# Feed-forward matmuls of a two-block transformer on one core: two matmuls of 256 columns, high weight part by high and by low activations, become one of 512

## The chip, the cores and the metric

The kernel runs on one core of a Trainium2 chip. The metric is the device time of one execution in microseconds (us); the median of several runs is given. TensorE does the matmuls (PE in the profile, its weight loads PEld), VectorE (DVE) and ScalarE (ACT) the elementwise work, GpSimd (POOL) a little of it, and the queue of SyncE (SP) starts nearly all DMA transfers.

## What is computed

Two transformer blocks follow each other, each of two layers, at model width 1024. All values are fp32. The second block works on the latents `x` (256 tokens) and on a context of 256 tokens, which its first layer carries along; its last layer updates the latents alone.

```
def first_block(x, ...):
    for l in range(2):
        h = rms_norm(x, norm_mix_pre[l])
        x = x + rms_norm(hybrid_mixer(h, ...), norm_mix_post[l])
        h = rms_norm(x, norm_ffn_pre[l])
        x = x + rms_norm(swiglu(h, w_ffn_in[l], w_ffn_out[l]), norm_ffn_post[l])
    return x

def swiglu(h, w_in, w_out):
    g, up = jnp.split(h @ w_in, 2, axis=-1)
    return (jax.nn.silu(g) * up) @ w_out

def conv_ffn(h, P):                      # feed-forward part of second_block
    gt = dwconv(h @ P["w_gate"], P["ffn_conv_w"], P["ffn_conv_b"])
    return (jax.nn.silu(gt) * (h @ P["w_val"])) @ P["w_down"]
```

The hidden width of each feed-forward part is 2816, or 22 groups of 128. The second block also needs `silu(c) @ w_mod`, six rows of 1024 for each layer, from 24 MB of weights a layer.

## The kernel before

**Products in parts.** An fp32 product is made of three matmuls in a narrower format. Every weight tile `raw` (128 x 1024, 512 KB) is split into a rounded high part `hi` and the remainder `lo`; so are the activations (`hThi`, `hTlo`). `mm3` issues high by high (L508), high by low (L509) and low by high (L510) into one PSUM accumulator. In the rows below the right-hand side of an arrow names the moving operand and the weights: `mm<-hTlo,hi` is L509.

**The weight stream.** `Stream` brings one 128 x 1024 tile for each projection, in the order of use. The load goes out on SP's queue (L262, six `raw` buffers), ACT makes `hi` (L275) and DVE makes `lo` (L278); there are four buffers each for `hi` and `lo`. The split is issued three tiles ahead, so that the `lo` of tile k + 3 stands on DVE's list near the work of projection k.

**The feed-forward input.** `ffn_in` goes over the 22 hidden groups. For each it makes two projections, `g` and `up`: 8 steps of 128 along the model width, three matmuls of 256 columns each step. Both 256-token results share one PSUM bank of 512 columns. `swiglu_unit` turns them into the hidden values: a tanh on ACT (L833), two operations on DVE (L834, L835, tile `tt`), and the split into `hh` (ACT, L840) and `hl` (DVE, L841). `convffn_unit`, in the second block, does the same with a convolution of three taps.

Three stages have this form with 256 tokens: the first block's layer 0 (406 to 546 us of the trace, called f1 below), its layer 1 (1035 to 1183 us, f2) and the second block's layer 1 (1963 to 2091 us, s1). Each has 44 projections, called P0 to P43. The second block's layer 0 works on 512 tokens and has 512-column matmuls already.

**What else runs in them.** In f1 and f2 the generator `mods` is woven in. It multiplies the `w_mod` tiles (`wm`, two buffers, loaded on SP's queue at L1142) by a column of the condition, and adds them up on DVE in two accumulators `macc` (L1169 for the first tile of a row, L1171 for the seven others; four instructions of 512 columns for each tile). When the eight tiles of a row are added, PE sums over the partitions (`am`, L1177), transposes (L1187), and DVE writes the result to `kept` (L1190); rows 2 and 5 then go to DRAM as `md`, in DMAs on POOL's queue (L1195). In f2 attention and a convolution of the second block's context run too (`cv`, `on`, `cn`, `yl`).

**What sets the order.** The program is written as above; a scheduler then puts the instructions of each engine in one fixed list, by readiness and priority. Every engine works through its list in that order and waits on semaphores, so an instruction that waits holds up all that stand behind it. PSUM's eight banks are handed out by the same scheduler.

Of the kernel before, what the change touches and what calls it, by code (L numbers as in the profile page):

```python
# [10 lines left out]
FR = mybir.dt.float32r  # L11
AF = mybir.ActivationFunctionType
# [121 lines left out]
class Pack:  # L134
    def __init__(self):
        self.at = {}
        self.n = 0
        self.items = []
# [160 lines left out]
class Kern:  # L299
# [30 lines left out]
    def __init__(self, nc, tc, ctx, dr, stop=None):  # L330
        self.nc, self.tc, self.dr = nc, tc, dr
        self.stop = stop
        e = ctx.enter_context
        self.cp = e(tc.tile_pool(name="const", bufs=1))
        self.wp = e(tc.tile_pool(name="wts", bufs=4))
        self.sp = e(tc.tile_pool(name="slots", bufs=self.NSLOT))
        self.tp = e(tc.tile_pool(name="tmp", bufs=3))
        self.mp = e(tc.tile_pool(name="psmm", bufs=4, space=PSUM))
        self.ap = e(tc.tile_pool(name="psax", bufs=4, space=PSUM))
        self.dp = e(tc.tile_pool(name="scratch", bufs=1, space=bass.MemoryType.DRAM))  # L340
        self.x = self.cp.tile([128, 2, D], F32, name="x")
        self.xc = self.cp.tile([128, 2, D], F32, name="xc")
        cpk = const_params()
        kept = self.cp.tile([128, cpk.n + KEEP], F32, name="kept")
        self.kept, self.kept_n = kept, 0
        self.ident, cst, self.tabs, self.ctp, self.ct, self.ones, self.nh, self.par_f = (
            self.keep(n) for n in (128, cpk.n, 512, 256, 16, 1, 1, 240))
        self.cst_all, self.cst = cst, {n: cpk.get(cst, n) for n in cpk.at}
        for t in range(2):
            for h in range(2):  # L350
                sl = slice(512 * h, 512 * h + 512)
                nc.sync.dma_start(self.x[:, t, sl], dr["x"][128 * t:128 * t + 128, sl])
        nc.sync.dma_start(self.ident, dr["ident"])
        nc.gpsimd.memset(self.ones, 1.0)
        nc.gpsimd.memset(self.nh, -0.5)
        self.par = {}
        self.uid = 0
        self.lanes = [[] for _ in range(7)]
        self.lo_pool = 0
        self.front = []  # L360
        self.P2, self.late, self.ctx_out, self.tails = None, [], {}, []
        self.filler, self.filled = None, 0
        layers = [(dr[f"w_f{l}"], first_units(l)) for l in range(2)] + [(dr[f"w_s{l}"], second_units(l)) for l in range(2)]
        self.st = Stream(self, layers)
# [70 lines left out]
    def norm_acts(self, ntok):  # L435
        per = 1024 // ntok
        out = []
        for _ in range(8 // per):
            hi, lo = self.slot("hThi", FR), self.slot("hTlo", FR)
            for k in range(per):  # L440
                o = slice(ntok * k, ntok * k + ntok)
                out.append((hi[:, o], lo[:, o]))
        return out
# [68 lines left out]
    def proj_T(self, key, ps, acts, nk=8, width=128, m=0, part=None):  # L512
        hi, lo = self.st.next(key) if part is None else part
        for k in range(nk):
            o = k * width + 128 * m
            self.mm3(ps, (hi[:, o:o + 128], lo[:, o:o + 128]), acts[k], k == 0, k == nk - 1)

    def proj_T_held(self, keys, pss, acts, order):
        parts = [self.st.next(key, hold=True) for key in keys]
# [282 lines left out]
    def ffn_in(self, hT, part, fn, side=1):  # L802
        ntok = hT[0][0].shape[-1]
        per = 1024 // ntok
        hid, hi, lo = [], None, None
        done = {}
        if ntok == 512 and part[0] == 0:
            done = {("g", 0): self.mm_ps(), ("up", 0): self.mm_ps(), ("g", 1): self.mm_ps()}
            self.proj_T_held(list(done), list(done.values()), hT, (1, 0))
        for i, m in enumerate(part):  # L810
            if i % per == 0:
                hi, lo = self.slot("hh", FR), self.slot("hl", FR)
            pg = done.get(("g", m)) or self.mm_ps()
            pu = done.get(("up", m)) or (pg[:, 256:] if ntok == 256 else self.mm_ps())
            pg = pg[:, :ntok]
            if ("g", m) not in done:
                self.proj_T(("g", m), pg, hT)
            if ("up", m) not in done:
                self.proj_T(("up", m), pu, hT)
            o = slice(ntok * (i % per), ntok * (i % per) + ntok)  # L820
            fn(m, pg, pu, hi[:, o], lo[:, o])
            hid.append((hi[:, o], lo[:, o]))
            self.run_side(side)
            if ntok == 512:
                self.fill(2 if self.filled < 64 else 3)
            elif i % 4 < 3 and self.filled < 48:
                self.fill(1)
        return hid
# [993 lines left out]
```

## Time and profile before

| | |
|---|---|
| median of 3 runs | 2151.7 us (2150.6 to 2153.8) |
| profiled execution | 2158.38 us, span 2156.2 us |
| mean granted TensorE clock | 0.983 of full speed |
| PE busy | 2071.8 us, 96% of the span |
| DVE busy | 1557.3 us, 72% |
| ACT busy | 1070.1 us, 50% |
| f1, f2, s1: first to last matmul | 406.05 to 546.24, 1034.98 to 1183.07, 1963.42 to 2091.38 us |

The span reaches from the first instruction to the last one; the profiled execution took 2.2 us more than that, and 6.7 us more than the median. The shares are means over stages that differ, so the rows of one stage say more than the table.

### The profile page before, as it was taken

Reading aid. Unit: us, or ns where it says so; the run is one execution under the profiler, and the core shown is the slowest. Engines: PE = TensorE matmul, PEld = TensorE weight load, DVE = VectorE, ACT = ScalarE, POOL = GpSimd, SP = SyncE. Lnnn points to the kernel's source line nnn. Section 1 sums busy time; section 2 is a strip of 40 time slices with the busy share of each in tenths; the row PEclk is TensorE's granted clock in tenths of the full one; section 3 lists DMA queues with packets and bytes.
Section 4 is the critical chain, followed back from the end, with each engine's and each line's share of the span. In section 5 each row is a group of like instructions: output and inputs, shape, how many; then the busy total and the mean of one; then the engine's idle time right before and its main releaser. Section 6 shows DMA issues by size and latency. Waiting matters only on the chain.

```text
span 2156.2 us, 34229 instructions
## 1 busy us (share of the span) xinstructions
PE 2071.8 (96%) x13088; PEld 1801.9 (84%) x13088; DVE 1557.3 (72%) x2823; ACT 1070.1 (50%) x1900; POOL 293.8 (14%) x271
## 2 busy tenths in 40 slices
PE   8999999999999999999799987999989999899999
PEld 6788899898887898998799876687868888678997
DVE  7756656897579466569997489789865546977774
ACT  5555644644455556457545474643313335455552
POOL 2101112100032011121300045100000002610000
PEclk9999999999999999999899999899999999999999
DMA  8545566687655454557566744256873233324553
GB/s 308 159 137 174 179 199 196 208 233 252 201 175 165 147 157 130 174 169 251 158 204 170 249 139 152 100 158 196 232 226 107 73 105 108 97 83 144 186 186 117
DMA packets 102356, 366.67 MB, mean 170 GB/s; under 512 B 12560, under 2 KB 12720, under 8 KB 102192
## 3 DMA queue, kind: packets, MB, share of 16 engines
q1 hardware_dynamic: 99920, 358.65, 52.8%
q0 software_dynamic: 2272, 5.83, 1.0%
q8 instruction: 103, 1.69, 0.3%
q14 instruction: 61, 0.50, 0.1%
HBM read 361.76 MB, written 2.68 MB: 169 GB/s over the span
## 4 chain that ended last, share of the span: by engine, by line
PE 84%; DVE 9%; DMA 3%; issue 2%; ACT 1%; POOL 0%; SPq 0%; POOLq 0%; DVEq 0%; ACTq 0%
PE mm L508 25%; PE mm L510 25%; PE mm L509 25%; DMA wm<-in_w_mod 2%; DVE cv L1504 2%; DVE lo L278 2%; DVE macc L1171 2%; PE ax L1312 1%; PE ax L937 1%; PE ax L1342 1%; ACT hi L275 1%; PE am L1158 1%; PE ay L461 1%; PE ay L590 1%; PE ax L892 1%
## 5 line engine op out<-in xcount | busy, mean ns | idle before, releaser
L275 ACT ACTIVATE hi<-raw 128x1024 fp32r<-128x1024 f32 (+1 forms) x564 | 592.9, 1054 | 765.8 <-PE mm L509 382.1
L278 DVE TENSOR_TENSOR lo<-raw,hi 128x1024 fp32r<-128x1024 f32 (+2 forms) x552 | 694.7, 1261 | 373.8 <-ACT hi L275 366.6
L508 PE MATMUL mm<-hThi,hi 128*128 128x256 f32 (+1 forms) x2408 | 723.1, 302 | 14.6 <-DVE gz L1291 12.1
L510 PE MATMUL mm<-hThi,lo 128*128 128x256 f32 (+1 forms) x2408 | 717.2, 299 | 4.6 <-DVE lo L278 4.5
L509 PE MATMUL mm<-hTlo,hi 128*128 128x256 f32 (+1 forms) x2408 | 719.6, 300 | 0.5 <-DVE hTlo L471 0.5
L508 PEld LDWEIGHTS mm<-hThi,hi 128*128 128x128 f32 x2408 | 460.2, 192 | 44.6 <-issue 13.6
L510 PEld LDWEIGHTS mm<-hThi,lo 128*128 128x128 f32 x2408 | 461.0, 192 | 24.2 <-DVE lo L278 5.0
L509 PEld LDWEIGHTS mm<-hTlo,hi 128*128 128x128 f32 x2408 | 462.5, 192 | 15.3 <-issue 1.7
L509 PE MATMUL mm<-lo,hThi 128*128 128x512 f32 (+2 forms) x480 | 182.4, 381 | 9.7 <-DVE lo L278 9.7
L508 PE MATMUL mm<-hi,hThi 128*128 128x512 f32 (+2 forms) x480 | 181.7, 386 | 5.2 <-DVE rb L579 3.1
L1171 DVE SCALAR_TENSOR_TENSOR macc<-wm,kept,macc 128x512 f32<-128x512 f32 x224 | 161.8, 763 | 31.5 <-DMA wm<-in_w_mod 31.3
L510 PE MATMUL mm<-hi,hTlo 128*128 128x512 f32 (+2 forms) x480 | 180.2, 378 | 0.0
L508 PE MATMUL mm<-hi,hh 128*128 128x512 f32 x440 | 173.1, 394 | 4.2 <-DVE xn L1564 4.2
L509 PE MATMUL mm<-lo,hh 128*128 128x512 f32 x440 | 173.2, 394 | 3.1 <-DVE lo L278 3.1
L510 PE MATMUL mm<-hi,hl 128*128 128x512 f32 x440 | 172.6, 393 | 0.0
L509 PEld LDWEIGHTS mm<-lo,hThi 128*128 128x128 f32 x480 | 90.9, 190 | 28.3 <-DVE lo L278 12.4
L508 PEld LDWEIGHTS mm<-hi,hThi 128*128 128x128 f32 x480 | 90.9, 190 | 26.4 <-issue 6.9
L510 PEld LDWEIGHTS mm<-hi,hTlo 128*128 128x128 f32 x480 | 90.5, 189 | 16.3 <-issue 0.3
L508 PEld LDWEIGHTS mm<-hi,hh 128*128 128x128 f32 x440 | 83.6, 190 | 22.4 <-issue 5.0
L509 PEld LDWEIGHTS mm<-lo,hh 128*128 128x128 f32 x440 | 83.7, 190 | 21.0 <-DVE lo L278 3.6
L510 PEld LDWEIGHTS mm<-hi,hl 128*128 128x128 f32 x440 | 83.7, 190 | 17.7
L1504 DVE SCALAR_TENSOR_TENSOR cv<-yp,kept,cv 128x256 f32<-128x256 f32 x120 | 85.1, 713 | 2.1 <-ACT cv L1500 0.7
(355 smaller groups left out, 2789.4 us busy)
## 6 DMA issues: line engine op xcount, KB each, us to landing
raw<-in_w_f SPq DMA_DIRECT2D x364, 512.0 KB, 4.1
raw<-in_w_s SPq DMA_DIRECT2D x190, 512.0 KB, 3.8
wm<-in_w_mod SPq DMA_DIRECT2D x96, 512.0 KB, 4.4
bc<-csd POOLq DMA_DIRECT2D x32, 128.0 KB, 5.8
mrow<-md SPq DMA_DIRECT2D x6, 512.0 KB, 4.3
row<-in_rows SPq DMA_DIRECT2D x4, 512.0 KB, 5.7
raw<-in_w_f SPq DMA_DIRECT2D x4, 510.0 KB, 4.8
par<-in_par_s SPq DMA_DIRECT2D x2, 918.5 KB, 8.3
```

Source lines behind the costliest of these rows:

```text
L275: nc.scalar.activation(hi[:, :n], raw[:, :n], AF.Copy)
L278: ins = eng.tensor_sub(lo[:, :n], raw[:, :n], hi[:, :n].bitcast(F32)).ins
L461: nc.tensor.transpose(pss[k // 2][:, o:o + 128], xs[k // 4][:, 128 * (k % 4):128 * (k % 4) + 128], self.ident)
L508: nc.tensor.matmul(ps, ah, bh, start=first, stop=False)
L509: nc.tensor.matmul(ps, ah, bl, start=False, stop=False)
L510: nc.tensor.matmul(ps, al, bh, start=False, stop=last)
L590: nc.tensor.transpose(ps[:, b * 256 + t * 128:b * 256 + t * 128 + 128], nat[t][:, (b0 + b) * 128:(b0 + b) * 128 + 128], self.ident)
L892: nc.tensor.matmul(pair[j][:, 128:384], q[j][:, 128:], k[j], start=True, stop=True)
L937: nc.tensor.matmul(ps[64 * j:64 * j + 64, 0:256], vv, pt[:, 0:256], start=True, stop=False, skip_group_check=True)
L1158: nc.tensor.matmul(ps[32 * j:32 * j + 32, :256], self.ctp[:, 32 * kk:32 * kk + 32], loaded[i - k + kk][:, 256 * j:256 * j + 256], start=kk ...
L1171: nc.vector.scalar_tensor_tensor(sums[w][:, o], loaded[i][:, o], c, sums[w][:, o], op0=ALU.mult, op1=ALU.add)
L1504: nc.vector.scalar_tensor_tensor(c, y[:, j:j + 256], wj, c, op0=ALU.mult, op1=ALU.add)
```

## The change

For 256 tokens `norm_acts` lays the high and the low part of the activations side by side (`hThl`, 512 columns for each step). A new `proj_wide` gives the high weight part both at once, as one matmul of 512 columns (L530 of the changed kernel), and the low weight part the high activations (L531, 256 columns). The left half of the accumulator then holds high by high and low by high, the right half high by low. A new `halves` adds them: ACT copies the right half to an SBUF tile `pair` (L535), and DVE adds the left half to it (L536). `g` and `up` take a PSUM bank each, and the units read SBUF tiles where they read PSUM. Lines behind these move down, so that in the changed kernel `macc` is at L1195 and L1197, `am` at L1203, `kept` at L1216, `tt` at L860 and L861 and `hl` at L867.

```diff
--- before.py
+++ after.py
@@ -354,7 +354,7 @@
         nc.gpsimd.memset(self.ones, 1.0)
         nc.gpsimd.memset(self.nh, -0.5)
         self.par = {}
-        self.uid = 0
+        self.uid, self.wide = 0, {}
         self.lanes = [[] for _ in range(7)]
         self.lo_pool = 0
         self.front = []
@@ -435,6 +435,13 @@
     def norm_acts(self, ntok):
         per = 1024 // ntok
         out = []
+        if ntok == 256:
+            for _ in range(4):
+                both = self.slot("hThl", FR)
+                for k in range(2):
+                    out.append((both[:, 512 * k:512 * k + 256], both[:, 512 * k + 256:512 * k + 512]))
+                    self.wide[id(out[-1])] = (out[-1], both[:, 512 * k:512 * k + 512])
+            return out
         for _ in range(8 // per):
             hi, lo = self.slot("hThi", FR), self.slot("hTlo", FR)
             for k in range(per):
@@ -514,6 +521,20 @@
         for k in range(nk):
             o = k * width + 128 * m
             self.mm3(ps, (hi[:, o:o + 128], lo[:, o:o + 128]), acts[k], k == 0, k == nk - 1)
+
+    def proj_wide(self, key, ps, acts):
+        hi, lo = self.st.next(key)
+        nc, nk = self.nc, len(acts)
+        for k, act in enumerate(acts):
+            o = slice(128 * k, 128 * k + 128)
+            nc.tensor.matmul(ps, hi[:, o], self.wide[id(act)][1], start=k == 0, stop=False, skip_group_check=True)
+            nc.tensor.matmul(ps[:, :256], lo[:, o], act[0], start=False, stop=k == nk - 1, skip_group_check=True)
+
+    def halves(self, ps):
+        v = self.tmp("pair", 256)
+        self.nc.scalar.activation(v, ps[:, 256:], AF.Copy)
+        self.nc.vector.tensor_add(v, ps[:, :256], v)
+        return v
 
     def proj_T_held(self, keys, pss, acts, order):
         parts = [self.st.next(key, hold=True) for key in keys]
@@ -811,12 +832,17 @@
             if i % per == 0:
                 hi, lo = self.slot("hh", FR), self.slot("hl", FR)
             pg = done.get(("g", m)) or self.mm_ps()
-            pu = done.get(("up", m)) or (pg[:, 256:] if ntok == 256 else self.mm_ps())
-            pg = pg[:, :ntok]
-            if ("g", m) not in done:
-                self.proj_T(("g", m), pg, hT)
-            if ("up", m) not in done:
-                self.proj_T(("up", m), pu, hT)
+            pu = done.get(("up", m)) or self.mm_ps()
+            if ntok == 256:
+                self.proj_wide(("g", m), pg, hT)
+                pg = self.halves(pg)
+                self.proj_wide(("up", m), pu, hT)
+                pu = self.halves(pu)
+            else:
+                if ("g", m) not in done:
+                    self.proj_T(("g", m), pg, hT)
+                if ("up", m) not in done:
+                    self.proj_T(("up", m), pu, hT)
             o = slice(ntok * (i % per), ntok * (i % per) + ntok)
             fn(m, pg, pu, hi[:, o], lo[:, o])
             hid.append((hi[:, o], lo[:, o]))
```

The scheduler's lists change too. On PE, in the middle of s1, six rows of a projection stood as follows before, two steps of the sum.

```order
L508 MATMUL mm_2220_20753<-hThi_2138_19687,hi_520_20644 128x256
L509 MATMUL mm_2220_20753<-hTlo_2139_19688,hi_520_20644 128x256
L510 MATMUL mm_2220_20753<-hThi_2138_19687,lo_520_20645 128x256
L508 MATMUL mm_2220_20753<-hThi_2136_19685,hi_521_20685 128x256
L509 MATMUL mm_2220_20753<-hTlo_2137_19686,hi_521_20685 128x256
L510 MATMUL mm_2220_20753<-hThi_2136_19685,lo_521_20686 128x256
```

In the changed kernel six rows of the same projection are three steps.

```order
L530 MATMUL mm_2385_20258<-hThl_2268_19289,hi_520_20163 128x512
L531 MATMUL mm_2385_20258<-hThl_2268_19289,lo_520_20164 128x256
L530 MATMUL mm_2385_20258<-hThl_2269_19290,hi_520_20163 128x512
L531 MATMUL mm_2385_20258<-hThl_2269_19290,lo_520_20164 128x256
L530 MATMUL mm_2385_20258<-hThl_2269_19290,hi_520_20163 128x512
L531 MATMUL mm_2385_20258<-hThl_2269_19290,lo_520_20164 128x256
```

There are 12080 rows on PE before and 11023 after; the three matmuls of a step have become two.

In f1 the sum over the partitions for row 3 of `w_mod` (`am<-macc0_3`) stands on PE's list like this before. The weights `hi_146` and `lo_146` belong to P35, `hi_147` to P36; the first tile of P0 is number 111.

```order
L509 MATMUL mm_590_5869<-hTlo_509_4535,hi_146_5798 128x256
L510 MATMUL mm_590_5869<-hThi_508_4534,lo_146_5799 128x256
L1177 MATMUL am_604_6161<-macc0_3_0_5427,kept_77 32x256 x2
L508 MATMUL mm_593_5943<-hThi_506_4532,hi_147_5828 128x256
L509 MATMUL mm_593_5943<-hTlo_507_4533,hi_147_5828 128x256
L1177 MATMUL am_604_6161<-macc0_3_0_5427,kept_77 32x256 x2
L1177 MATMUL am_604_6161<-macc0_3_1_5428,kept_77 32x256 x2
```

In the changed kernel, where `hi_136` belongs to P25 and `hi_137` to P26:

```order
L530 MATMUL mm_610_5396<-hThl_509_4535,hi_136_5338 128x512
L531 MATMUL mm_610_5396<-hThl_509_4535,lo_136_5339 128x256
L1203 MATMUL am_667_5972<-macc0_3_0_5328,kept_77 32x256 x2
L530 MATMUL mm_615_5460<-hThl_506_4532,hi_137_5363 128x512
L531 MATMUL mm_615_5460<-hThl_506_4532,lo_137_5364 128x256
```

The sum has moved from between P35 and P36 to between P25 and P26. On DVE's list of the changed kernel the first half of that accumulator is finished here, in its row with `wm0_3_7`:

```order
L1197 SCALAR_TENSOR_TENSOR macc0_3_1_5329<-wm0_3_6_5775,kept_77,macc0_3_1_5329 128x512
L861 SCALAR_TENSOR_TENSOR tt_591_5238<-tt_591_5238,pair_589_5234 128x256
L278 TENSOR_TENSOR lo_138_5400<-raw_138_5294,hi_138_5399 128x1024
L860 SCALAR_TENSOR_TENSOR tt_600_5320<-th_599_5319,pair_597_5291 128x256
L1197 SCALAR_TENSOR_TENSOR macc0_3_0_5328<-wm0_3_7_5840,kept_77,macc0_3_0_5328 128x512
L536 TENSOR_TENSOR pair_603_5358<-mm_601_5334,pair_603_5358 128x256
L1197 SCALAR_TENSOR_TENSOR macc0_3_0_5328<-wm0_3_7_5840,kept_77,macc0_3_0_5328 128x512
L1197 SCALAR_TENSOR_TENSOR macc0_3_1_5329<-wm0_3_7_5840,kept_77,macc0_3_1_5329 128x512
L278 TENSOR_TENSOR lo_139_5425<-raw_139_5336,hi_139_5424 128x1024
```

`lo_138` and `lo_139` belong to P27 and P28. Before, `lo_146` stood ahead of the same accumulation, so that it has moved up past eight `lo`.

In f2, `lo_335` (P35) and `lo_336` (P36) stood on DVE's list of before like this (`cn` and `lrs` are of the context's convolution):

```order
L278 TENSOR_TENSOR lo_335_13058<-raw_335_12941,hi_335_13057 128x1024
L1524 TENSOR_SCALAR cn_1278_12134<-cn_1278_12134,lrs_1280_12136 128x256
L414 TENSOR_SCALAR lrs_1283_12146<-csum_1282_12145 128x1
L278 TENSOR_TENSOR lo_336_13088<-raw_336_12985,hi_336_13087 128x1024
L1524 TENSOR_SCALAR cn_1278_12134<-cn_1278_12134,lrs_1283_12146 128x256
```

In the changed kernel 30 rows stand between the two; these are the last of them, up to `lo_336`.

```order
L536 TENSOR_TENSOR pair_1474_12610<-mm_1472_12586,pair_1474_12610 128x256
L536 TENSOR_TENSOR pair_1475_12635<-mm_1473_12587,pair_1475_12635 128x256
L861 SCALAR_TENSOR_TENSOR tt_1471_12574<-tt_1471_12574,pair_1469_12570 128x256
L860 SCALAR_TENSOR_TENSOR tt_1477_12639<-th_1476_12638,pair_1474_12610 128x256
L536 TENSOR_TENSOR pair_1480_12675<-mm_1478_12651,pair_1480_12675 128x256
L861 SCALAR_TENSOR_TENSOR tt_1477_12639<-tt_1477_12639,pair_1475_12635 128x256
L536 TENSOR_TENSOR pair_1481_12700<-mm_1479_12652,pair_1481_12700 128x256
L867 TENSOR_TENSOR hl_1458_12446<-tt_1471_12574,hh_1457_12445 128x256
L860 SCALAR_TENSOR_TENSOR tt_1483_12704<-th_1482_12703,pair_1480_12675 128x256
L867 TENSOR_TENSOR hl_1458_12446<-tt_1477_12639,hh_1457_12445 128x256
L861 SCALAR_TENSOR_TENSOR tt_1483_12704<-tt_1483_12704,pair_1481_12700 128x256
L867 TENSOR_TENSOR hl_1458_12446<-tt_1483_12704,hh_1457_12445 128x256
L278 TENSOR_TENSOR lo_336_12742<-raw_336_12653,hi_336_12741 128x1024
```

The others of the 30 are the normalisation of the context's attention (`or`, `on`), `cn`, `lrs`, two `cv`, five `yl`, one `tt` and five more `hl`. Before, `or`, `on`, `cv`, `yl` and the `hl` all stood behind `lo_336`.

## Rows read from the trace of the kernel before

**Rows 1.** The page: part 1, and the granted clock in 40 slices

```profile
PE 2071.8 (96%) x13088; PEld 1801.9 (84%) x13088; DVE 1557.3 (72%) x2823; ACT 1070.1 (50%) x1900; POOL 293.8 (14%) x271
...
PEclk9999999999999999999899999899999999999999
```

**Rows 2.** Windows: length, busy us (instructions) by engine, clock, DMA share, GB/s

```profile
406.00:482.00 76.00, 75.42 (x623) 73.53 (x624) 74.16 (x120) 36.43 (x58) 8.71 (x6) 1.00 0.79 232
482.00:496.00 14.00, 9.48 (x80) 9.28 (x78) 3.79 (x8) 4.26 (x6) 0.00 (x0) 0.91 0.67 169
496.00:546.00 50.00, 49.98 (x398) 48.35 (x399) 42.09 (x67) 21.95 (x35) 0.00 (x0) 0.96 0.77 255
546.00:617.00 71.00, 71.00 (x317) 58.76 (x316) 39.23 (x44) 34.80 (x47) 5.61 (x6) 1.00 0.62 188
1035.00:1150.00 115.00, 114.35 (x919) 109.12 (x920) 112.87 (x225) 58.90 (x126) 13.65 (x15) 0.98 0.63 200
1963.00:2091.00 128.00, 128.00 (x1057) 127.90 (x1056) 96.58 (x163) 71.88 (x114) 0.00 (x0) 0.98 0.56 178
```

**Rows 3.** Timeline of PE: start, us, operation; in s1, then in a feed-forward output

```profile
2016.06 0.28 PE L509 MATMUL mm<-hTlo,hi 128*128 128x256 f32 x1
...
2022.14 0.28 PE L509 MATMUL mm<-hTlo,hi 128*128 128x256 f32 x1
...
559.64 0.39 PE L510 MATMUL mm<-hi,hl 128*128 128x512 f32 x1
...
565.76 0.39 PE L510 MATMUL mm<-hi,hl 128*128 128x512 f32 x1
```

**Rows 4.** DVE's groups in s1: busy us, mean ns, idle before and releaser

```profile
L278 DVE TENSOR_TENSOR lo<-raw,hi 128x1024 fp32r<-128x1024 f32 x44 | 53.9, 1225 | 30.7 <-ACT hi L275 30.6
```

**Rows 5.** Timeline of DVE in f1: its first `lo`, and a stretch without idle time

```profile
416.05 1.22 DVE L278 TENSOR_TENSOR lo<-raw,hi 128x1024 fp32r<-128x1024 f32 x1
...
450.34 2.07 DVE L1171 SCALAR_TENSOR_TENSOR macc<-wm,kept,macc 128x512 f32<-128x512 f32 x3
452.33 1.21 DVE L278 TENSOR_TENSOR lo<-raw,hi 128x1024 fp32r<-128x1024 f32 x1
453.47 0.41 DVE L834 SCALAR_TENSOR_TENSOR tt<-th,mm 128x256 f32<-128x256 f32 x1
453.80 0.41 DVE L835 SCALAR_TENSOR_TENSOR tt<-tt,mm 128x256 f32<-128x256 f32 x1
454.13 0.74 DVE L1171 SCALAR_TENSOR_TENSOR macc<-wm,kept,macc 128x512 f32<-128x512 f32 x1
```

**Rows 6.** DVE's groups in f1, the filler

```profile
L1171 DVE SCALAR_TENSOR_TENSOR macc<-wm,kept,macc 128x512 f32<-128x512 f32 x56 | 40.2, 745 | 10.2 <-DMA wm<-in_w_mod 10.2
```

**Rows 7.** Timelines of POOL, DVE and PE, the chain, and the page's DMA issues

```profile
469.85 1.81 POOL L1195 DMA_DIRECT2D md<-kept  x2 [35.73 <-DVE kept L1190]
...
493.41 1.42 DVE L1171 SCALAR_TENSOR_TENSOR macc<-wm,kept,macc 128x512 f32<-128x512 f32 x2 [10.21 <-DMA wm<-in_w_mod]
...
496.02 0.58 PE L510 MATMUL mm<-hThi,lo 128*128 128x256 f32 x1 [4.54 <-DVE lo L278]
...
475.16 18.15 DMA wm<-in_w_mod
...
wm<-in_w_mod SPq DMA_DIRECT2D x96, 512.0 KB, 4.4
```

**Rows 8.** Timeline of DVE in the last part of f2

```profile
1146.03 1.23 DVE L278 TENSOR_TENSOR lo<-raw,hi 128x1024 fp32r<-128x1024 f32 x1
...
1163.06 0.69 DVE L1359 TENSOR_TENSOR on<-ax,or 128x512 f32<-128x512 f32 x1
...
1168.51 1.76 DVE L841 TENSOR_TENSOR hl<-tt,hh 128x256 fp32r<-128x256 f32 x5
```

**Rows 9.** Timeline of PE: first matmul behind f1, and behind f2

```profile
546.24 0.40 PE L508 MATMUL mm<-hi,hh 128*128 128x512 f32 x1
...
1183.07 0.40 PE L508 MATMUL mm<-hi,hh 128*128 128x512 f32 x1
```

## Prediction

> **What bounds the kernel now.** I read the page's first part, then windows over the three stages that change, then the timelines of PE and DVE in them. The page shows a kernel that TensorE bounds: PE is busy for 2071.8 of 2156.2 us, at full clock in all but one of 40 slices [rows 1]. That is an average. The windows show three different stages [rows 2]. In s1 PE is busy for all 128 us while DVE has 96.6 us of work. There DVE's idle time stands ahead of `lo`, where it waits for ACT's `hi` [rows 4]; it is kept waiting, it keeps nobody. In f1 DVE is busy for 74.2 of the first 76 us, and in f2 for 112.9 of the first 115. PE is busy there too: the two are nearly level, with 56 `macc` of 40.2 us [rows 6] in f1 between the weight splits. And in f1 there is one place where DVE has already lost: a `wm` tile comes 10.2 us late, and PE then waits 4.5 us for the next `lo` [rows 7]. What DVE gets as extra work should cost nothing in s1, and most of its price in f1 and f2.
>
> **The PE term.** In s1 51 matmuls of 256 columns follow each other from 2016.06 to 2022.14, 0.119 us each; I use 0.120. In a feed-forward output 27 of 512 columns take from 559.64 to 565.76, 0.2267 each [rows 3]. A step of three small matmuls takes 0.360 us; the new step takes 0.2267 + 0.120 = 0.3467. That saves 0.0133 us a step, 0.107 a projection (2.88 becomes 2.77), 4.7 us for 44 projections, 14.1 us for the three stages if PE stays the bound. So a matmul carries about 13 ns that don't depend on its columns. The Trainium skill ("TensorE: Matmul & The Clock Gate", section "Back-to-back issue gap") gives the gap as columns / 2.4 + 2.5 ns, and by it a step would save 2.5 ns only, 0.9 us a stage; it speaks against the change, and the forecast would be 3.8 us later by it, through s1. The trace's spacing for both sizes in this kernel differs from that rule, so I keep the trace's.
>
> **The ACT term.** 44 copies a stage. ACT is busy for 36.4 of f1's first 76 us, and even at its mean of 0.63 us an instruction there [rows 2] the copies would add 28 us to the 63 that it has in 140. Hidden, at nothing; what they do is to delay the adds and the tanh by one step.
>
> **The DVE term.** 44 adds a stage. The nearest row is `tt`, 256 columns with one operand in PSUM: it starts 0.33 us ahead of the next one in a stretch without idle time. In the same stretch `lo` takes 1.14 and `macc` 0.663 (1.99 for three) [rows 5]. The units' operations now read SBUF where they read PSUM; `hl`, which reads SBUF alone, takes 0.34 (five in 1.76 us [rows 8]), the same as `tt`, so nothing is gained there. So DVE gets 14.6 us a stage. In s1 that is 96.6 + 14.6 = 111.2 of 123 us: still hidden, and s1 ends 4.7 us earlier.
>
> **f1.** Everything on DVE ahead of 416.05 is the same in both lists. Behind it, up to the first half of `macc0_3_0` with `wm0_3_7` in the changed list, there stand 24 `lo` (27.3), 49 `macc` of L1197 (32.5), 22 adds (7.3), 30 `tt` and `hl` (10.0) and eight others (3.0): 80.1 us, to 496.1 [rows 5]. The same sum over the list of before meets its trace within 0.1 us wherever DVE doesn't idle. PE's list has `am` between P25 and P26 now, and `am` needs that row. So P26 can't start before 496.4; before, PE stood at P28 at 496.0 [rows 7]. From there 18 projections of 2.77 and `am` take 50.5, to 546.9, 0.7 later than the 546.2 of before [rows 9]. That is without a wait for `wm`, and I don't expect to be without one. Before, the `md` transfers went out at 469.85, and a `wm` load behind them, issued at 475.16, took 18.15 us where the median is 4.4 [rows 7]: it landed 23 us after `md`. In the changed list `kept` moves up ahead of most of the row-3 `macc`. The sum puts it at 461.8, with `md` right behind, the release of the buffer for `wm0_3_3` at 463.1, and the first use of that tile at 470.8. A load that goes out at 463 and lands 18 us later comes at 481, 10 us late. All the `macc` and `lo` behind it wait, and PE with them. f1: +0.7 + 10 = +11, between +0.7 (loads undisturbed) and +17 (landing 23 us after `md`, and half clock after the gap, which cost 4% of 50 us before [rows 2]).
>
> **f2.** Up to `lo_335` the changed list has 28 adds more (9.3 us), and 0.8 us of other rows have moved behind it. That `lo` ended at 1147.3 before [rows 8], and so comes at 1155.8. Then 30 rows stand ahead of `lo_336`, where two stood: 18 of `tt`, `hl` and adds (6.0), seven `yl` and `cv` (2.5), the attention's norm and `cn` (1.2), and `lo_336` itself (1.1), 10.8 us in all, with up to 1.6 us in which the norm waits for other engines. Before, the norm and the `hl` came behind, at 1163.06 and 1168.51 [rows 8]. P36 gets its low weights at about 1167.5; eight projections take 22.2, to 1189.7, against 1183.1 [rows 9]: +6.6. `md` of row 5 moves up into the stage as well; six raw buffers cover most of that stall, and I take 1.5 of 0 to 3. f2: +8, between +4 (if the slack in its first half takes in half of the adds) and +13.
>
> **Behind them.** The feed-forward output of f1 has PE busy for 71.0 of 71 us and DVE for 39.2 [rows 2], so it passes the shift on in full and makes up for nothing.
>
> **Sum.** +11 + 8 - 4.7 = +14.3 on a span of 2156.2. The profiled execution, 2158.4 with what lies around its span, is 6.7 over the median, and I put the same sum on the median: 2151.7 + 14.3 = 2166.0.
>
> **Rivals.** *The adds are hidden and PE decides everywhere:* -14.1, 2137.6. It holds where DVE's work stays below 2.77 us a projection. For it: s1. Against it: f1 had 74.2 + 3.8 + 42.1 = 120 us of DVE work in its 140 [rows 2], and 134.6 with the adds, against 122 of PE. Chance 6%. *The idle time of before takes the adds in:* f1 has 20 us of it. If the `wm` loads come in time, f1 is +0.7, f2 +4, s1 -4.7: 2151.7, no change. For it: DVE gets to `wm0_3_7` no later than before. Against it: the idle time is a wait for a load, and the load's stall moves up with `kept`. Chance 22%, with a quarter of it on the faster side. *More is lost than the sum says:* f1 +17, f2 +13, s1 -2 for want of a PSUM bank or because of ACT's step: +28, 2180. For it: PE's clock stood at 0.91 in the window with the gap [rows 2], and several gaps would be several of these. Chance 20%. *The 512-column step saves nothing:* s1 is level, and the time 2171; that lies within my forecast's own range.
>
> **How the numbers follow.** The forecast has 52%, with a range of its own from 2160 to 2172. To leave out no more than two in ten, the range goes down to the case without a late load, 2150, and up to the third rival, 2182. Faster by over 0.2% (4.3 us, about what a measurement of this kernel can tell from no change) has 6% from the first rival and 4% from the second: 10%. Within 0.2%: 15%, from the second. Slower: 75%.
>
> **What would show it.** PE's spacing at L530 and L531 of 0.227 and 0.120, and s1 123 us long with DVE idle ahead of `lo`: the PE term. DVE without idle time from 416 on, a `macc` that waits about 10 us for `wm` near 471, and `am` (L1203) waiting for DVE near 506: f1. PE waiting at L531 for `lo` some 5 us or more ahead of P36: f2. The forecast is wrong if the `wm` loads behind `md` land in time, if an add takes much less than 0.33 us, or if s1 has PE waits for `pair`.

## The result, and the profile after

The changed kernel takes 2188.6 us (median of 4 runs, 2186.4 to 2189.7), against 2152.75 (2150.6 to 2153.8): 1.0161 times the time of before, 95% interval 1.0147 to 1.0175. It is 36 us slower, where 14 were forecast and the range ended at 2182. The direction was right, and the size was not.

The page's first part shows that the change did to PE what its arithmetic says: 1056 matmuls fewer (8 for each of the 132 projections), and 4 us less busy time; DVE has 44 us more.

```profile
PE 2067.8 (95%) x12032; PEld 1746.0 (80%) x12032; DVE 1601.4 (73%) x2955; ACT 1111.0 (51%) x2032; POOL 293.4 (13%) x271
```

The three stages, from their first matmul to the first of the feed-forward output behind them, read from PE's timeline:

| | before | after | difference | forecast |
|---|---|---|---|---|
| f1 | 140.2 | 158.9 | +18.7 | +11 |
| f2 | 148.1 | 169.4 | +21.3 | +8 |
| s1 | 128.0 | 124.6 | -3.4 | -4.7 |

They sum to +36.6, and the medians differ by 35.9. The spans of the two profiled executions differ by 31.5 only: the stretch from f2's end to the next feed-forward output, which the change doesn't touch, took 363.4 us in the one of before and 357.1 in this one. It took 356 to 367 in the executions of all the kernels below, so the stages are compared, not the spans.

The windows over the three stages, and over the end of a stall in f1 (the second), read like [rows 2]: busy us by engine, the granted clock, DMA share, GB/s.

```profile
407.00:566.00 159.00, 136.12 (x746) 114.14 (x747) 134.69 (x234) 75.99 (x141) 8.38 (x6) 0.92 0.72 206
483.00:500.00 17.00, 10.89 (x50) 9.20 (x51) 14.69 (x25) 6.55 (x12) 0.00 (x0) 0.73 0.88 259
1053.00:1223.00 170.00, 151.53 (x844) 125.00 (x845) 153.65 (x319) 92.07 (x209) 16.49 (x18) 0.94 0.57 168
1998.00:2122.00 124.00, 123.83 (x700) 107.99 (x700) 105.29 (x196) 82.14 (x151) 0.00 (x0) 0.99 0.54 182
```

PE, without a pause in f1 before but for one, is now busy for 136 of 159 us there and 151.5 of 170 in f2; in s1 it has no pause. The granted clock is 0.73 over the window in which PE starts again.

**s1.** PE's timeline, ten projections apart (160 rows):

```profile
2030.43 0.40 PE L530 MATMUL mm<-hThl,hi 128*128 128x512 f32 x1
...
2058.45 0.40 PE L530 MATMUL mm<-hThl,hi 128*128 128x512 f32 x1
```

28.02 us for 80 steps is 0.3503 a step, where three matmuls took 0.3576 [rows 3]. DVE's groups in s1 show that the adds are hidden: `lo` still waits for `hi`, 18.7 us instead of 30.7 [rows 4].

```profile
L278 DVE TENSOR_TENSOR lo<-raw,hi 128x1024 fp32r<-128x1024 f32 x44 | 53.9, 1225 | 18.7 <-ACT hi L275 18.7
...
L536 DVE TENSOR_TENSOR pair<-mm,pair 128x256 f32<-128x256 f32 x41 | 15.5, 416 | 0.0
```

**f1.** The waits in it: engine, line and tile that waited, for what; us in total, times, the longest.

```profile
PE mm L531 <- DVE lo L278: 14.4, 3, 13.0
...
DVE macc L1197 <- DMA wm<-in_w_mod: 13.6, 2, 13.2
...
PE am L1203 <- DVE macc L1197: 5.1, 2, 4.7
```

The timelines of POOL and DVE show the stall of before [rows 7] at its new place, 7 to 9 us earlier and longer.

```profile
462.95 1.81 POOL L1221 DMA_DIRECT2D md<-kept  x2 [31.78 <-DVE kept L1216]
...
484.89 1.41 DVE L1197 SCALAR_TENSOR_TENSOR macc<-wm,kept,macc 128x512 f32<-128x512 f32 x2 [13.18 <-DMA wm<-in_w_mod]
```

And the chain of f1 shows what held it: a `wm` load that took 20.8 us behind the `md` transfers, `macc` and `lo` one after another, then `am`, then P26.

```profile
464.01 20.79 DMA wm<-in_w_mod
...
510.77 1.07 PE am L1203 x4
...
511.83 0.73 PE mm L530
```

**f2.** PE's timeline without the projections' own rows, at P31:

```profile
1175.70 0.60 PE L1545 MATMUL az<-kept,cv 128*128 128x128 f32 x4
1177.66 0.61 PE L1368 MATMUL ax<-cvv,at 128*128 128x128 f32 x4
1179.72 0.30 PE L1556 MATMUL az<-kept,cn 128*128 128x128 f32 x1 [1.45 <-DVE cn L1550]
1182.95 1.08 PE L1393 MATMUL ax<-kept,on 128*128 128x128 f32 x4 [2.94 <-DVE on L1385]
1183.83 0.84 PE L1556 MATMUL az<-kept,cn 128*128 128x128 f32 x3
...
1187.65 0.80 PE L530 MATMUL mm<-hThl,hi 128*128 128x512 f32 x1 [2.97 <-DVE yl L1398]
```

From 1177.66 to 1187.65 rows of attention and convolution, called the tail below, follow each other with no projection between. They need answers of DVE, ACT and POOL to the ones before them. P31 took 13.9 us where 2.8 is its length, and P32 behind it 4.9, with a granted clock of 0.51 from 1187.65 to 1192.20. Before, the same rows stood apart, with projections between:

```profile
1137.86 0.61 PE L1342 MATMUL ax<-cvv,at 128*128 128x128 f32 x4
...
1159.70 0.27 PE L1530 MATMUL az<-kept,cn 128*128 128x128 f32 x1
...
1165.35 0.60 PE L1367 MATMUL ax<-kept,on 128*128 128x128 f32 x4
```

DVE's rows at P31 and behind it: `on`, for which PE waits at 1182.95, and the `lo` that I had taken for the bound.

```profile
1182.12 0.69 DVE L1385 TENSOR_TENSOR on<-ax,or 128x512 f32<-128x512 f32 x1
...
1195.77 1.23 DVE L278 TENSOR_TENSOR lo<-raw,hi 128x1024 fp32r<-128x1024 f32 x1 [0.53 <-ACT hi L275]
```

That `lo` (`lo_336`) was ready at 1196.9, and P36 began at 1200.9: it held up nothing. PE waited for no low weights in f2. What it did wait for, ahead of the tail, was the adds, five times between 1093 and 1133:

```profile
PE mm L530 <- DVE pair L536: 7.6, 5, 2.7
```

Each time it is the first matmul of a projection. That one reads nothing that an add writes; what the two share is a PSUM tile `mm`, which the add has still to read. So PE stood for want of a PSUM bank.

The `md` transfers of row 5 went out at 1148.91 here. A `raw` load behind them took 20.5 us, and DVE waited 3.3 us for `hi` just ahead of the tail. In e2 below that wait was 0.9 us, and P31 still took 12.9.

### The profile page after: what moved, and what is told of

Its sections match the earlier page's. It is cut to its first block, busy times and chain, and to the rows that moved or that the text cites. A ratio compares the mean times of both kernels' runs of the same rounds, so it can differ in the third digit from the quotient of the medians.

```text
span 2187.7 us, 32405 instructions
## 1 busy us (share of the span) xinstructions
PE 2067.8 (95%) x12032; PEld 1746.0 (80%) x12032; DVE 1601.4 (73%) x2955; ACT 1111.0 (51%) x2032; POOL 293.4 (13%) x271
## 4 chain that ended last, share of the span: by engine, by line
PE 74%; DVE 17%; DMA 4%; issue 3%; ACT 2%; POOL 0%; DVEq 0%; SPq 0%; POOLq 0%; ACTq 0%
PE mm L515 18%; PE mm L517 18%; PE mm L516 18%; PE mm L530 8%; DVE macc L1197 5%; DVE lo L278 4%; PE mm L531 4%; DMA wm<-in_w_mod 3%; DVE cv L1530 2%; PE ax L1338 1%; PE ax L963 1%; DMA raw<-in_w_f 1%; ACT hi L275 1%; PE ax L1368 1%; PE am L1184 1%
## 5 line engine op out<-in xcount | busy, mean ns | idle before, releaser
L530 PE MATMUL mm<-hThl,hi 128*128 128x512 f32 x1056 | 385.1, 407 | 25.0 <-DVE gz L1317 12.1
L531 PE MATMUL mm<-hThl,lo 128*128 128x256 f32 x1056 | 301.3, 286 | 14.4 <-DVE lo L278 14.4
L515 PE MATMUL mm<-hThl,hi 128*128 128x256 f32 x928 | 267.5, 290 | 1.0 <-DVE hThl L482 1.0
L530 PEld LDWEIGHTS mm<-hThl,hi 128*128 128x128 f32 x1056 | 203.8, 193 | 79.6 <-DVE gz L1317 12.3
L516 PE MATMUL mm<-hThl,hi 128*128 128x256 f32 x928 | 263.4, 285 | 0.0
L517 PE MATMUL mm<-hThl,lo 128*128 128x256 f32 x928 | 262.2, 285 | 0.0
L531 PEld LDWEIGHTS mm<-hThl,lo 128*128 128x128 f32 x1056 | 205.0, 194 | 15.8 <-DVE lo L278 15.3
L1197 DVE SCALAR_TENSOR_TENSOR macc<-wm,kept,macc 128x512 f32<-128x512 f32 x224 | 162.7, 763 | 37.0 <-DMA wm<-in_w_mod 36.7
L515 PEld LDWEIGHTS mm<-hThl,hi 128*128 128x128 f32 x928 | 177.7, 192 | 13.3 <-issue 10.3
L516 PEld LDWEIGHTS mm<-hThl,hi 128*128 128x128 f32 x928 | 178.4, 192 | 1.7 <-issue 1.7
L517 PEld LDWEIGHTS mm<-hThl,lo 128*128 128x128 f32 x928 | 177.5, 192 | 2.6 <-issue 1.7
L516 PE MATMUL mm<-hTlo,hi 128*128 128x512 f32 (+1 forms) x424 | 154.7, 366 | 0.0
L515 PE MATMUL mm<-hThi,hi 128*128 128x512 f32 (+1 forms) x424 | 153.7, 367 | 1.1 <-ACT nv L481 1.1
L517 PE MATMUL mm<-hThi,lo 128*128 128x512 f32 (+1 forms) x424 | 154.5, 366 | 0.0
L516 PE MATMUL mm<-lo,hThl 128*128 128x512 f32 (+2 forms) x384 | 145.4, 380 | 7.8 <-DVE lo L278 7.8
L515 PE MATMUL mm<-hi,hThl 128*128 128x512 f32 (+2 forms) x384 | 145.4, 387 | 1.0 <-ACT hThl L477 0.8
L517 PE MATMUL mm<-hi,hThl 128*128 128x512 f32 (+2 forms) x384 | 143.9, 378 | 0.0
## 6 DMA issues: line engine op xcount, KB each, us to landing
bc<-csd POOLq DMA_DIRECT2D x32, 128.0 KB, 5.1
```

The costliest lines, as they stand in the source:

```text
L515: nc.tensor.matmul(ps, ah, bh, start=first, stop=False)
L516: nc.tensor.matmul(ps, ah, bl, start=False, stop=False)
L517: nc.tensor.matmul(ps, al, bh, start=False, stop=last)
L530: nc.tensor.matmul(ps, hi[:, o], self.wide[id(act)][1], start=k == 0, stop=False, skip_group_check=True)
L531: nc.tensor.matmul(ps[:, :256], lo[:, o], act[0], start=False, stop=k == nk - 1, skip_group_check=True)
L1197: nc.vector.scalar_tensor_tensor(sums[w][:, o], loaded[i][:, o], c, sums[w][:, o], op0=ALU.mult, op1=ALU.add)
```

## The experiments

Theory at the start: the adds are too much for DVE in f1 and f2, so PE waits there. Rivals: the wide matmuls, the banks or the lists cost by themselves; the loads behind `md` cost, not DVE's work. Stage lengths of one execution each, in us; the ratio is to the kernel before, with its interval. The kernel before varied by more on the chips of these runs (2147 to 2162), so stage lengths tell most. Where kernels share the lists of a stage, f2 repeats within 0.3 us and s1 within 0.7; f1, with its stall, only within 4.5 (changed and e5).

| | f1 | f2 | s1 | ratio |
|---|---|---|---|---|
| before | 140.2 | 148.1 | 128.0 | |
| changed | 158.9 | 169.4 | 124.6 | 1.0161 (1.0147 to 1.0175) |
| e1 wide in s1 alone | 141.8 | 148.1 | 124.5 | 0.9996 (0.9982 to 1.0011) |
| e2 wide, no adds | 138.4 | 159.0 | 124.7 | 1.0034 (1.0020 to 1.0047) |
| e3 narrow, with adds | 158.9 | 172.1 | 128.0 | 1.0198 (1.0173 to 1.0222) |
| e5 `md` later (not moved) | 154.4 | 169.1 | 124.7 | 1.0135 (1.0115 to 1.0155) |
| e6 adds on GpSimd | 152.4 | 170.6 | 124.7 | 1.0138 (1.0117 to 1.0159) |
| e7 narrow, copies, no adds | 139.9 | 156.7 | 127.6 | 1.0055 (1.0035 to 1.0076) |
| e8 changed, tail spread | 159.2 | 159.0 | 125.2 | 1.0132 (1.0099 to 1.0166) |
| e9 e6, tail spread | 152.5 | 156.6 | 124.6 | 1.0092 (1.0064 to 1.0119) |
| e10 no adds, tail spread | 139.5 | 149.7 | 124.7 | 1.0003 (0.9986 to 1.0019) |
| e11 less filler in f1 | 145.0 | 182.4 | 124.7 | 1.0161 (1.0141 to 1.0182) |
| e12 e1, `md` later (not moved) | 140.3 | 148.2 | 124.6 | 0.9996 (0.9981 to 1.0012) |
| e13 changed, `md` later | 144.2 | 171.4 | 124.5 | 1.0115 (1.0088 to 1.0142) |
| e14 e1, `md` later | 133.6 | 148.1 | 124.6 | 0.9986 (0.9971 to 1.0000) |
| e15 e1, `md` at f1's end | 133.6 | 148.1 | 125.0 | 0.9975 (0.9965 to 0.9985) |

**e1: the wide form in s1 alone.**

```diff
-        hT = self.norm_acts(256 * ng)
+        hT = self.norm_acts(256 * ng, ng == 1)    # hThl only where asked for
...
-            if ntok == 256:
+            wide = id(hT[0]) in self.wide
+            if wide:
```

> The wide form in s1 alone; f1 and f2 keep the three matmuls and their lists, row for row. Theory (the loss comes from DVE's extra work in the two stages where DVE has none to spare): f1 and f2 last 140 and 148 us as before, s1 ends 3.5 us earlier than before, and the time is about 2149, 3.5 under the kernel before. Rival (the wide form only moves work to DVE, and what s1 gains is given back behind it): s1 is shorter but the whole is within 1 us of before, 2152.

s1 was 3.5 us shorter, f2 as before and f1 1.6 longer with the same lists, much as the theory has it. The whole is within the noise of these runs, so the time alone doesn't show the gain.

**e2: wide, without the adds.**

```diff
-        self.nc.scalar.activation(v, ps[:, 256:], AF.Copy)
-        self.nc.vector.tensor_add(v, ps[:, :256], v)
+        self.nc.scalar.activation(v, ps[:, :256], AF.Copy)
```

> Wide matmuls everywhere, but the right half isn't added: ACT copies the left half out, and DVE has no add. (High weights times low activations are left out of the result.) Theory of DVE's extra work: f1 and f2 no longer than before, each some 2.5 us shorter as s1 is, and the time near 2145, with f1 within 136 to 141 and f2 within 144 to 149. Rival (the wide matmuls, the two PSUM banks and the new lists cost, not the adds): f1 and f2 stay above 150 and 158, and the time above 2170.

For f1 the theory is right: without adds 138.4, all of the loss gone. For f2 it fails: 159.0, still 11 over before without a single add. In s1 124.7 without adds and 124.6 with them: there they cost nothing. PE's timeline in f2 showed the same row of transposes at P31:

```profile
1152.01 0.44 PE L1555 MATMUL az<-kept,cn 128*128 128x128 f32 x1 [2.07 <-issue]
...
1153.61 1.08 PE L1392 MATMUL ax<-kept,on 128*128 128x128 f32 x4 [1.16 <-issue]
...
1154.49 0.84 PE L1555 MATMUL az<-kept,cn 128*128 128x128 f32 x3
```

**e3: three narrow matmuls, with the adds.**

```diff
-            nc.tensor.matmul(ps, hi[:, o], self.wide[id(act)][1], ...)
+            nc.tensor.matmul(ps[:, :256], hi[:, o], act[0], start=k == 0, ...)
+            nc.tensor.matmul(ps[:, 256:], hi[:, o], act[1], start=k == 0, stop=k == nk - 1, ...)
```

(The values that this kernel computes differ from the others'; its instructions and their sizes are those named.)

> The three matmuls of 256 columns as before, but with the high by low product in the right half of a bank of its own, so that the copies and adds of the changed kernel stay. Theory of DVE's extra work: f1 and f2 as long as in the changed kernel, 159 and 169, within 5 us; s1 back to 128; the time near 2192, 2185 to 2198. Rival (the wide matmuls cost, the adds are hidden): f1 and f2 near 140 and 148, the time within 5 us of 2153.

f1 lost as much as in the changed kernel without any wide matmul, and s1 lost its gain. The wide matmul isn't what costs.

**e5 and e12: `md` later, by where it is written.**

```diff
-                if r in (2, 5):
-                    nc.gpsimd.dma_start(md[which, r // 3, :]..., col[:, which, :])
+                if r in (2, 5):
+                    late.append((md[which, r // 3, :]..., col[:, which, :]))
+            if l or r == 5:
+                while late:
+                    nc.gpsimd.dma_start(*late.pop(0))
```

> The changed kernel with the two md transfers of row 2 issued with those of row 5, in f2, so that none goes out in f1. Theory (the 13 us in which DVE waits for wm at 472 to 485 in f1 are the loads behind md, and PE stands still in them): the wait is gone, f1 lasts 145 to 150 instead of 159, f2 up to 4 us longer than 169.5 for four transfers instead of two, and the time 2174 to 2182. Rival (DVE is the bound of f1 anyway, and the wait only takes the place of work that is late): f1 stays above 155, the time above 2184.

> The wide form in s1 alone, and the md transfers of row 2 issued with those of row 5. f1 and f2 keep the lists of before but for those transfers. Theory: f1 loses the 10 us wait of DVE and the 4.5 us of PE behind it, with the half clock after it, and lasts 134 to 136 instead of 140; f2 148 to 152; s1 124.6; the time 4 to 9 us under the kernel before. Rival (the loads that were late in f1 are late in f2 instead): f1 shorter, f2 longer by as much, the time within 3 us of before.

Neither moved anything: the scheduler put the transfers where their data was ready, at 463.50 in e5, and the lists of PE and DVE were those of the changed kernel and of e1.

```profile
463.50 1.81 POOL L1224 DMA_DIRECT2D md<-kept  x2 [32.91 <-DVE kept L1216]
```

So these two say nothing of the stall; they are repeats, e5 of the changed kernel and e12 of e1. As such they show that the stall varies: DVE waited 10.3 us for `wm` in e5 and 13.2 in the changed kernel's execution, and f1 was 4.5 us shorter.

**e6: the adds on GpSimd.**

```diff
-        self.nc.vector.tensor_add(v, ps[:, :256], v)
+        u = self.tmp("pair", 256)
+        self.nc.scalar.activation(u, ps[:, :256], AF.Copy)
+        self.nc.gpsimd.tensor_tensor(v, u, v, op=ALU.add)
```

> The changed kernel with the adds taken off DVE: ACT copies both halves out, GpSimd adds them. Theory (in f1 DVE's time is what counts; in f2 half the loss is the adds and half the place of the context's attention tail on PE's list, which stands in one piece at P31 here too): f1 138 to 143, f2 156 to 162, s1 124.7 as with the adds on DVE, the time near 2162. Rival (the chain copy, add, tanh is what holds the stages up, on whatever engine): f1 above 150, f2 above 165, the time above 2178.

f1 was 152.4 and f2 170.6, which are the rival's numbers. But in f1 its mechanism isn't what the trace shows: PE waited there for `lo` (15.6 us) and never for `pair`. DVE had no adds and was still late. Its groups from 407 to 545 us (mean ns of one behind the comma), first of e6, then of the changed kernel:

```profile
L278 DVE TENSOR_TENSOR lo<-raw,hi 128x1024 fp32r<-128x1024 f32 x38 | 49.2, 1297 | 0.0
L1199 DVE SCALAR_TENSOR_TENSOR macc<-wm,kept,macc 128x512 f32<-128x512 f32 x56 | 46.8, 869 | 9.7 <-DMA wm<-in_w_mod 9.7
L1197 DVE TENSOR_SCALAR macc<-wm,kept 128x512 f32<-128x512 f32 x12 | 7.3, 646 | 0.0
```

```profile
L278 DVE TENSOR_TENSOR lo<-raw,hi 128x1024 fp32r<-128x1024 f32 x36 | 43.8, 1217 | 4.2 <-ACT hi L275 4.0
...
L1197 DVE SCALAR_TENSOR_TENSOR macc<-wm,kept,macc 128x512 f32<-128x512 f32 x56 | 39.8, 741 | 13.6 <-DMA wm<-in_w_mod 13.6
...
L1195 DVE TENSOR_SCALAR macc<-wm,kept 128x512 f32<-128x512 f32 x12 | 5.2, 481 | 1.1 <-PE am L1203 1.1
```

`lo` took 80 ns longer, `macc` 128 and 165, the three operations of a hidden group 62 to 87 each. Over f1's 44, 56, 12 and 66 of them that is 3.5 + 7.2 + 2.0 + 4.7 = 17 us, more than the 14.6 that the adds were. GpSimd was busy with its adds for 58 us of the stage:

```profile
L538 POOL TENSOR_TENSOR pair<-pair,pair 128x256 f32<-128x256 f32 x43 | 57.9, 1353 | 89.3 <-ACT pair L537 86.0 <-PE mm L531 1.6 <-DVE lo L278 1.2
```

So DVE's time in f1 was no less than with the adds, and for f1 e6 speaks for the theory rather than against it. The Trainium skill ("SBUF — State Buffer", section "Who interferes with whom") says that a DVE instruction with two SBUF inputs contends with a GpSimd instruction that reads SBUF. `lo`, `tt`, `hl` and `macc` of L1199 have two and were slower beside these adds; the trace agrees. `macc` of L1197, with one tile and a column, was slowed most, by 165 ns, and that sentence doesn't cover it.

**e7: narrow, with the copies and banks, no adds.** On top of e2:

```diff
-            nc.tensor.matmul(ps, hi[:, o], self.wide[id(act)][1], ...)
+            nc.tensor.matmul(ps[:, :256], hi[:, o], act[0], start=k == 0, ...)
+            nc.tensor.matmul(ps[:, :256], hi[:, o], act[1], start=False, ...)
```

> Three matmuls of 256 columns into one half, a bank for each projection, ACT's copy to SBUF and no add: the banks and the copies of the changed kernel without its wide matmuls. The attention tail stands at P29, P31 and P33 on PE's list, with projections between its parts. Theory (tail in one piece costs f2 10 us): f1 140 to 142, f2 148 to 154, s1 128, the time within 5 us of before. Rival (banks and copies cost f2 its 10 us): f2 158 or more, the time 10 over before.

f2 was 156.7, nearer to the rival. The order had the tail in pieces, but close together, and P29 to P33 took 25.3 us where 14.4 is their length: 10.9, more than f2's whole excess of 8.6. Whether banks and copies cost by themselves, or only through the list they led to, is told by e10.

**e8: the changed kernel, tail spread.**

```diff
-        hid = self.ffn_in(hT, range(NH), self.swiglu_unit, side=2 if l else 1)
+        hid = self.ffn_in(hT, range(NH), self.swiglu_unit, side=1 if l else 1)
```

> The changed kernel with one step of side work for each hidden group of f2 instead of two, which spreads the tail of the context's attention over P33 to P43 on PE's list. Theory (of f2's 21 us some 10 are PE waiting in the tail at P31): f2 159 to 164 instead of 169.4, unless the last pieces at P43 wait as long; f1 159 and s1 124.6 unchanged. Rival (DVE's 14.6 us more set f2, wherever the tail stands): f2 168 or more.

f2 was 159.0, 10.4 less, as the theory has it, and PE no longer waited in the tail; 7.2 us of waits for `pair` stayed. PE's timeline shows its pieces apart, with projections between:

```profile
1180.33 0.27 PE L1393 MATMUL ax<-kept,on 128*128 128x128 f32 x1
...
1186.75 0.38 PE L1358 MATMUL ax<-kept,dp 128*128 128x128 f32 x2
...
1191.72 0.27 PE L1556 MATMUL az<-kept,cn 128*128 128x128 f32 x1
...
1194.03 0.49 PE L1556 MATMUL az<-kept,cn 128*128 128x128 f32 x3
```

A part of the gain is work that left the stage: four `ax<-cvv,at` and four `on` transposes, and 2.0 us of DVE's rows, now stand behind f2, and the feed-forward output there took 1.0 us more. The whole gained little in this execution: 5.3 us were lost ahead of s1, where PE's rows were the same and the granted clock was 0.95, not 0.99. e9 and e10 have the same edit and didn't lose them.

**e10: no adds, tail spread.** e2 with the line of e8.

> Wide matmuls, copies but no adds (high weights times low activations are left out of the result), and one step of side work for each hidden group in f2, so that the attention tail is spread. Theory (f2's loss is 10 us of adds and 10 us of tail): f2 146 to 152 instead of 159.0 with the tail in one piece, f1 138 and s1 124.7 as without adds. Rival (the copies and the banks cost f2 about 10 us wherever the tail stands): f2 157 or more.

149.7. So of f2's 21.3 us the tail is 9.3 (e2 to e10) to 10.4 (changed to e8), the adds 9.3 (e10 to e8) to 10.4 (e2 to changed), and 1.6 is left for banks and copies, with what PE should have gained (3.4 in s1); how these come about stays open. Each way some 1 us of the tail's share is work that left the stage. PE's waits say the same: for `pair` and in the tail in the changed kernel, for `pair` alone in e8, in the tail (and 1.4 us for ACT's copies) in e2, for neither in e10. **e9**, with the adds on GpSimd and the tail spread, gave 156.6:

> The adds on GpSimd and the tail spread, both. Theory: f1 138 to 143, f2 148 to 154, s1 124.7, and the time 2 to 6 us under the kernel before. Rival (the tail's new place at P43 costs what P31 cost, or GpSimd is slower than ACT and DVE need): f2 above 157, the time 4 us or more over before.

f1 was 152.5 and the time 19 us over before, so the theory failed here: the tail is 14 us (e6 to e9), but what GpSimd costs DVE remains.

**e11: filler moved from f1 to f2.**

```diff
-            elif i % 4 < 3 and self.filled < 48:
+            elif i % 4 < 2 and self.filled < 48:
```

> The changed kernel, with filler behind two of four hidden groups in the first block instead of three: 48 macc in f1 and 66 in f2, where the changed kernel has 68 and 46. That takes 20 x 0.66 = 13 us of DVE's work out of f1 and puts it in f2. Theory (DVE's work decides in both stages): f1 141 to 147 instead of 159, f2 178 to 184 instead of 169, the time within 6 us of the changed kernel's. Rival (the wait for loads behind md and the lists decide, not the amount): f1 above 152, f2 below 174.

145.0 and 182.4, both as forecast: f1 gained 13.9 and f2 lost 13.0 with 13.3 us of DVE's work, and the time was that of the changed kernel. (By the trace f1 has 48 `macc` instead of 68, and f2 61 instead of 40.) These two stages are as long as what DVE has in them. The wait for `wm` was still 11.0 us.

**e13: `md` later, by its data.**

```diff
+            if l or r == 5:
+                for which, rr in late:
...
+                    if rr != r:    # row 2's column plus 0 times row 5's
...
+                        nc.vector.scalar_tensor_tensor(moved, col[:, which, :], 0.0, src[:, which, :], op0=ALU.mult, op1=ALU.add)
```

> The changed kernel, with the md transfers of row 2 made to depend on row 5's column (a DVE operation of 8 columns for each), so that they can't go out in f1; the lists of f1 are else the same. The edit e5 didn't move them: its transfers still went out at 463.5. Theory (the 10 to 13 us wait for wm is the loads behind md, and is lost on top of DVE's work): no such wait in f1, f1 141 to 148, f2 169 to 174 with four transfers, the time 2172 to 2180. Rival (the wait only takes the place of DVE work that is late anyway): f1 152 or more, the time above 2182.

Now they moved, and f1's lists are the same. DVE's waits from 406 to 560 us show none for `wm`:

```profile
DVE lo L278 <- ACT hi L275: 11.5, 18, 1.2
...
DVE macc L1195 <- PE am L1203: 0.9, 2, 0.5
```

f1 fell to 144.2, f2 was 171.4 and the time 2176.4, all as the theory has it. f1 is down by 14.7 from the changed kernel and by 10.2 from e5, its repeat. The `md` transfers are the cause of the wait, and all of it had been lost. PE's timeline shows `am` starting at the time that the prediction's sum gave for the case without a wait, 496.4:

```profile
496.37 1.07 PE L1203 MATMUL am<-macc,kept 128*32 128x256 f32 x4 [4.74 <-DVE macc L1197]
```

**e14 and e15: what could be kept.** The wide form in s1, and `md` moved as in e13; e15 makes row 2 depend on row 3's column instead of row 5's.

```diff
-            if l or r == 5:
+            if l or r in (3, 5):
```

> The wide form in s1 alone, with the same dependence of the row-2 transfers. Theory: f1 loses DVE's 10 us wait and PE's 4.5 with the slower clock behind it, 133 to 136 instead of 140; f2 148 to 152; s1 124.6; the time 4 to 9 us under the kernel before. Rival (f2, with four transfers, loses what f1 gains): the time within 3 us of before.

> The wide form in s1 alone, and the row-2 transfers made to depend on row 3's column, so that they go out at the end of f1, ahead of a feed-forward output in which each raw tile feeds 24 matmuls of 512 columns (5.4 us) and not 24 of 256 (2.9 us). The lists of PE and DVE are otherwise those of the wide form in s1 alone. Theory (a stall of the loads costs what six raw tiles don't cover, 17 us in a feed-forward input and 32 in an output): f1 133 to 136, the stretch behind f1 not longer, f2 148, s1 124.6, no loss behind f2, and the time 7 to 11 us under the kernel before. Rival (the loads' stall costs some 7 us wherever it falls): f1 shorter, the stretch behind it longer by 5 or more, the time within 4 us of before.

In both f1 lost the stall of before too, 6.6 us, and s1 its 3. Without the stall f1 is 133.6 with the matmuls of before and 144.2 in e13. So of the 18.7 us that f1 lost, 10.6 come of the adds and lists, less what the wide matmuls save, and 8.1 of the stall, which grew from 6.6 to 14.7. In e14 the loss came behind f2, as the rival has it: the feed-forward output there took 80.0 us instead of 75.2, with ACT waiting for raw tiles (15.4 us up to the next feed-forward output), as four transfers went out together. In e15 they went out at 534.67; PE lost 1.8 us in f1 and behind it, and the whole was faster than the kernel before, 2146.9 against 2153.5 (10 and 14 runs): 6.6 us, just short of the 7 to 11 expected.

```profile
534.67 1.81 POOL L1234 DMA_DIRECT2D md<-moved  x2 [100.61 <-DVE moved L1230]
```

```profile
PE mm L515 <- ACT hi L275: 1.0, 1, 1.0
...
PE mm L516 <- DVE lo L278: 0.8, 1, 0.8
```

## Why the prediction was wrong

**The PE term** was right where PE runs undisturbed in f2, and too large in s1. From P34 to P43 of f2 the new step took 0.3467 (72 steps in 24.96 us), and three matmuls took 0.360 there before (25 steps in 9.00 us):

```profile
1195.33 0.39 PE L530 MATMUL mm<-hThl,hi 128*128 128x512 f32 x1
...
1220.29 0.39 PE L530 MATMUL mm<-hThl,hi 128*128 128x512 f32 x1
```

```profile
1170.83 0.28 PE L508 MATMUL mm<-hThi,hi 128*128 128x256 f32 x1
...
1179.83 0.28 PE L508 MATMUL mm<-hThi,hi 128*128 128x256 f32 x1
```

In s1 the rows gave 0.3503 and 0.3576: 7 ns a step, not 13.3, and so 2.5 us for 352 steps, not 4.7. Why the two stages differ isn't shown. The other 0.9 of s1's 3.4 us lies in its first 7 us, where the granted clock was 0.65 before and is 0.80 now; no term of the sum had that. The Trainium skill ("TensorE: Matmul & The Clock Gate", section "Back-to-back issue gap") gives columns / 2.4 + 2.5 ns as the gap of an isolated matmul. By that a step saves an estimated 2.5 ns; the trace shows more in both stages.

**The ACT term, and the adds in s1,** were right there: with adds and without, s1 is 124.6 and 124.7. In f2 banks and copies left the loss named under e10.

**The DVE term** was right: an add takes 0.33 to the next start, as `tt` does, and e3, e2 and e11 show that in f1 the stage follows DVE's work.

**f1: the mechanism was right, two sizes were off.** The sum to 496.1 held (e13: 496.4). The wait for `wm` was 13.2 us and not 10, because the load took 20.8 us and not 18. And "18 projections of 2.77 and `am`", 50.5, took 55.7, from 510.77 to 566.47. PE stood idle nowhere in them. P26 took 5.6 us: from 511.8 to 516.3 the granted clock was 0.51, one step took 0.64 us, and a second part of `am` stands in it; a third makes P27 3.6; from P30 on a projection took 2.83. The range of the f1 term, up to 17, had the half clock in it, but not these.

**f2: the step that failed** is "P36 gets its low weights at about 1167.5". I read in DVE's list what stood ahead of `lo_336` and made that the bound of the stage. But the rows moved ahead of it, the attention's norm and `cn`, have readers on PE, and these stand in PE's list at P31, all together; before they were spread from P28 to P37. PE is held there by a chain over four engines, at a price of about 10 us (e8, e10), which DVE's busy time doesn't show. That is the term missing in the sum. The adds' part was 9.3 to 10.4, near the 8 that I had for the whole stage, but by another wait than I had: 7.6 us at the first matmul of five projections, for a bank that an add had still to read, and none for `lo`. Why the scheduler put the tail in one piece was not tried.

**The rivals.** That the idle time takes the adds in is refuted: the wait moved up with `kept` and was lost in full. That more is lost came nearest. The PSUM bank that it named for s1 was waited for in f2 (7.6 us) and never in s1, and the tail it didn't name.

## What to carry to other kernels

Work moved from a full engine to one that is nearly full in some stages is paid for stage by stage: ask where the receiver has time, and make the change there alone. When a change makes a scheduler rewrite its lists, compare every engine's list, and look on the waiting engine for chains that have lost the work between their links. An edit that should delay a transfer must change its data, or the scheduler undoes it; look in the trace whether it moved before reading the time.

## What was not expected of the hardware

Two transfers of 1024 four-byte elements on POOL's queue held up 512 KB loads on SP's: 18 to 21 us where the median is 4.4. Moving them to a stage that uses tiles half as fast took more out of f1 (6.6 us) than the wide form out of s1 (3.4). And GpSimd's adds of 1.35 us each made the DVE operations listed under e6 7 to 34% longer.
